# A depthwise convolution's taps dealt anew over VectorE, ScalarE with GpSimd, and TensorE in one trunk kernel

## The chip, the cores and the metric

One core of one Trainium2 chip runs the whole program. The metric is the device time of one launch in microseconds (us); lower is better. The program has no communication with other cores.

## The reference

The model is a trunk of two layers over 256 tokens of width 1024, in float32. Each layer is a half-step SwiGLU feed-forward block, a token mixer and a second feed-forward block, each with an RMSNorm ahead and behind it. The mixer of layer 0 is a convolution module, and the change lies in it alone:

```
u = h @ w_pw1 + b_pw1
u = u[..., :1024] * sigmoid(u[..., 1024:])
c = depthwise_conv(u, w_dw, width 31, centred) + b_dw     # per channel, 31 taps along the tokens
c = silu(layernorm(c, ln_g, ln_b))                        # over the 1024 channels of a token
return c @ w_pw2 + b_pw2
```

The mixer of layer 1 is differential attention. Feed-forward blocks are `(silu(h @ w_gate) * (h @ w_up)) @ w_down`.

## The kernel before

**Products.** Every float32 weight is split into two parts, hi and lo, that TensorE takes at its faster rate, and so is every activation; a product is three matmuls (`mm3`, lines 151 to 154). Weights arrive in jobs of half a megabyte (`issue`, line 107): SyncE starts a DMA into one of 5 `raw` buffers, ScalarE casts it into `wh` (line 113), VectorE subtracts into `wl` (line 114). Twelve split jobs are held (`NW`), and a job is started when the oldest of the twelve is freed, so weights are some three column pairs ahead of their use.

**Stages.** The trunk runs six sub-blocks in order, named a to f in the tile names: feed-forward, convolution (b), feed-forward, feed-forward, attention, feed-forward. The order of instructions on each engine is fixed when the program is built, by a scheduler; `after(...)` and `tc.high_priority()` steer it. Each engine then works strictly through its own list, and waits at the head of it.

**The convolution module** (`conv`, line 414). Channels are on partitions, 8 channel tiles of 128, tokens along the row; a tile is 128 x 256, with 15 zeros at either end so that a tap is a shifted slice.
- *pw1 and gate.* For each tile, TensorE makes a bank with both halves (tiles 0 to 3 through `px` and transposes `py`, tiles 4 to 7 in the two `gu` banks, line 241), ScalarE the sigmoid `sg` (line 439), VectorE `u` (line 450). A tile that TensorE will convolve is split into hi and lo (`us`, `split_to`, lines 272 and 273).
- *Taps of tiles 0 to 3 (`NDV = 4`)* on VectorE, two tiles in turn so that a tap never waits for the one ahead of it: one `tensor_scalar` (line 478) and 30 `scalar_tensor_tensor` (line 474) a tile, `co = u[shifted] * w + co`, all in SBUF: 120 of the latter.
- *Taps of tiles 4 to 7* on TensorE: for four taps at a time (a chunk) ScalarE makes four diagonal matrices of the hi weights (`dg`, line 495), GpSimd those of the lo weights with one `affine_select` (line 496), and TensorE multiplies (`mm3` into `cv`, line 502). There are 8 chunks a tile and three `dg` buffers. Building runs ahead of TensorE by those buffers.
- *LayerNorm sums.* From tiles 4 and 5 a rough mean of every token is taken (`shifts`, line 522), which all tiles are centred on (`centre`, lines 512 and 515); ScalarE squares them (`sq`, line 519). GpSimd adds the centred tiles and squares of five tiles into `sums` (lines 536, 537, 543, 544), VectorE those of the last three (line 552).
- *Statistics.* TensorE spins on 16 products that nobody reads (`w0`, line 232), then multiplies `sums` with ones into `pv` and `pm` (lines 557 and 559); VectorE and GpSimd make the factor, TensorE spreads it (line 172), with 6 and 6 further spins around it, and the bias rows of pw2 go into `accb` (line 287).
- *pw2.* VectorE normalises, ScalarE takes silu, the result is split and TensorE multiplies (`accb`).

PSUM has eight banks here: four `acc`, two `gu`, two `mi`. The centring of a tile stands at a chosen place in VectorE's list (after a tap of tile 3) and the square at a chosen place in ScalarE's (after a chunk of diagonals), which is all that decides what waits behind them:

```
with after(dve), tc.high_priority():
    ... V.tensor_tensor(c, c, shift, ALU.subtract)
sqs[ct] = hp.tile([P, S], F32, tag="sq", name=f"sq{ct}", bufs=2)
with after(act):
    A.activation(sqs[ct], c, AF.Square)
```

Of the kernel before, what the change touches and what calls it, by code (L numbers as in the profile page):

```python
# [18 lines left out]
P = 128  # L19
# [17 lines left out]
NDV = 4  # L37
# [12 lines left out]
def trunk_kernel(  # L50
# [83 lines left out]
    class Weight:  # L134
        """Some k tiles of a weight, in jobs of half a megabyte; w(k) gives hi and lo of tile k."""
# [30 lines left out]
    def spread(ms, rows, name):  # L166
        """rows[i] = ms[:, i]^-1/2, the same in every partition."""
        n = len(rows)
        rs = sp.tile([P, 2], F32, tag="rs2", name=f"rs{name}", bufs=2)
        G.tensor_tensor(rs[:, :n], ms, nhalf[:, :n], ALU.pow)  # L170
        for i in range(n):
            T.transpose(rows[i], rs[:, i:i + 1].to_broadcast([P, P]), ident)
# [55 lines left out]
    def spin(n, name):  # L228
        """n products that nobody reads: an idle tensor engine drops to half its clock."""
# [4 lines left out]
    def proj(w1, w2, f, name):  # L234
        """[w1 tile f | w2 tile f].T @ xT -> one bank [128, 2*S]."""
# [8 lines left out]
    def proj_x(pairs, order, name):  # L244
        """x[tb] @ [w1 | w2] for pairs of weights i, as (tb, i, bank [128 tokens, 2*FC])."""
# [15 lines left out]
    def projs(pairs, name):  # L261
        """(tile number, bank) of each pair of columns."""
# [12 lines left out]
    class Down:  # L275
        """y[tok, D] += s[:, tok].T @ W over k tiles; the tail one token block after the other."""
# [137 lines left out]
    def conv(hp, name):  # L414
# [22 lines left out]
        for ct, ps in lead():  # L437
            sg = sp.tile([P, S], F32, tag="sg", name=f"sg{name}{ct}")
            A.activation(sg, ps[:, 1, :], AF.Sigmoid, bias=par[:, 8 + ct:9 + ct])
            if ct < NDV:  # L440
                t = us[ct] = hp.tile([P, W], F32, tag="u", name=f"u{ct}", bufs=4)
                ends, u = [t], t[:, PAD:PAD + S]
            else:
                ends = ups[ct] = [hp.tile([P, W], F32R, tag="us", name=f"us{ct}{n}", bufs=8) for n in range(2)]
                u = sp.tile([P, S], F32, tag="hf", name=f"u{ct}")
# [5 lines left out]
            if ct >= NDV:  # L451
# [3 lines left out]
        # bias of pw2, as two rows (hi and lo) that its accumulators start with  # L455
# [9 lines left out]
        # taps of the first tiles on DVE, of the others as products with diagonals  # L465
        raw, tap = {}, {}
        for c0 in range(0, NDV, 2):
            for ct in (c0, c0 + 1):
                raw[ct] = hp.tile([P, S], F32, tag="co", name=f"co{ct}", bufs=NDV)
            for t in range(CONVW):  # L470
                for ct in (c0, c0 + 1):
# [4 lines left out]
                    else:  # L476
                        with after(tap[c0 - 1, CONVW - 1] if c0 else None):
                            V.tensor_scalar(c, u[:, 0:S], wdw[:, ct, 0:1], par[:, 16 + ct:17 + ct],
                                            ALU.mult, ALU.add)

        pm = ps_mi.tile([P, 512], F32, tag="mi", name="pm")
        pv = ps_mi.tile([P, 512], F32, tag="mi", name="pv")
        shift = hp.tile([P, S], F32, tag="shift", name="shift", bufs=1)
        sqs = {}

        built = {}

        def diagonals(ct, then=None):
            uh, ul = ups[ct]
            raw[ct] = ps_acc.tile([P, 512], F32, tag="acc", name=f"cv{ct}")[:, :S]  # L490
# [16 lines left out]

        def centre(ct, dve, act):
            with after(dve), tc.high_priority():
                if ct < NDV:  # L510
                    c = raw[ct]
                    V.tensor_tensor(c, c, shift, ALU.subtract)
                else:
                    c = hp.tile([P, W], F32, tag="us", name=f"co{ct}", bufs=8)[:, :S]
                    V.scalar_tensor_tensor(c, raw[ct], par[:, 16 + ct:17 + ct], shift, ALU.add, ALU.subtract)
            co[ct] = c
            sqs[ct] = hp.tile([P, S], F32, tag="sq", name=f"sq{ct}", bufs=2)
            with after(act):
                A.activation(sqs[ct], c, AF.Square)


        def shifts():
            # every token is centred on its mean over two tiles before its variance is taken
            for ct in (4, 5):
                e = sp.tile([P, S], F32, tag="hf", name=f"e{ct}")
                A.activation(e, raw[ct], AF.Identity, bias=par[:, 16 + ct:17 + ct])
                T.matmul(pm[:, S:], ones_d, e, start=ct == 4, stop=ct == 5)
            A.activation(shift, pm[:, S:], AF.Copy, scale=float(KD // 2))

        for ct in range(NDV, KD):  # L530
            diagonals(ct, shifts if ct == 6 else None)
        sums = [hp.tile([P, S], F32, tag=f"sum{n}", name=f"sum{n}", bufs=1) for n in range(2)]
        end = (CONVW - 1) // 4

        def add(ct, E):
            E.tensor_tensor(sums[0], sums[0], co[ct], ALU.add)
            E.tensor_tensor(sums[1], sums[1], sqs[ct], ALU.add)

        for ct, at, tp in ((4, (6, end), 10), (5, (6, end), 10), (0, (7, 1), 10), (1, (7, 1), 10), (6, (7, end), 24)):
            centre(ct, tap[3, tp], built[at][0])  # L540
            with after(built[at][1]):
                if ct == 5:
                    G.tensor_tensor(sums[0], co[4], co[5], ALU.add)
                    G.tensor_tensor(sums[1], sqs[4], sqs[5], ALU.add)
                elif ct != 4:
                    add(ct, G)
        centre(7, tap[3, CONVW - 1], built[7, end][0])
        for ct in (2, 3):
            centre(ct, None, built[7, end][0])
        for n, v in enumerate((co, sqs)):  # L550
            for ct in (7, 2, 3):
                V.tensor_tensor(sums[n], sums[n], v[ct], ALU.add)
# [237 lines left out]
```

## Time and profile before

| | |
|---|---|
| three runs | 1059.96, 1060.96, 1061.01 us; median 1060.96 |
| profiled execution, first to last instruction | span 1059.0 us |
| TensorE busy over the span | 1023.4 us (97%) |
| VectorE, ScalarE, GpSimd busy | 659.6, 553.7, 72.4 us |
| pw1's products end, diagonals begin | 258.97 us |
| first product of pw2 | 326.69 us |

The page gives one figure for the profiled execution, its span; the program's start and end lie around it, so a run of the same kernel is listed about 2 us above it. Spans, starts and lengths below are in us from the first instruction. A row "x30" is 30 instructions run together: its length is from the start of the first to the end of the last. In square brackets stands the idle time ahead of an instruction and what ended it.

### The profile page before, as it was taken

What the parts mean: (1) busy time and instruction counts of PE and PEld (TensorE: products, weight loads), DVE (VectorE), ACT (ScalarE), POOL (GpSimd) and SP (SyncE); (2) the same over time, 40 slices, a digit from 0 to 9 for tenths busy, and PEclk for the clock granted to TensorE, in tenths of its full rate; (3) what the DMA queues carried; (4) which work ended last, traced back from release to release, by engine and by line L of the source; (5) the groups of instructions that cost most, each with busy time, mean ns of one, the idle gap of its engine ahead of it and who ended that gap; (6) DMA issues with size and microseconds to landing.
All of it is one profiled execution on the core that took longest, in us unless ns stands there. A gap on an engine that the chain in (4) does not pass through costs nothing.

```text
span 1059.0 us, 17905 instructions
## 1 busy us (share of the span) xinstructions
PE 1023.4 (97%) x7133; PEld 947.7 (89%) x7133; DVE 659.6 (62%) x1007; ACT 553.7 (52%) x933; POOL 72.4 (7%) x110
## 2 busy tenths in 40 slices
PE   6999999999969999999999999999999999999997
PEld 5899999899967989999989999998899789999995
DVE  6655556679996755455575555566777685555542
ACT  6564445476845644444455445454577665445431
POOL 1000000031560100000010000001000110000000
PEclk9999999999998999999999999999999999999999
DMA  9877465376000666475555665554842255665511
GB/s 296 283 208 221 150 205 179 112 259 197 14 1 0 215 203 218 148 229 177 165 175 185 195 218 151 190 188 133 276 150 91 80 165 180 196 216 155 187 58 40
DMA packets 130492, 177.62 MB, mean 168 GB/s; under 512 B 6173, under 2 KB 112709, under 8 KB 130408
## 3 DMA queue, kind: packets, MB, share of 16 engines
q1 hardware_dynamic: 130408, 176.47, 52.1%
q8 instruction: 56, 0.92, 0.3%
q14 instruction: 28, 0.23, 0.1%
HBM read 175.40 MB, written 1.05 MB: 167 GB/s over the span
## 4 chain that ended last, share of the span: by engine, by line
PE 79%; DVE 10%; issue 3%; ACT 2%; DMA 2%; POOL 2%; SPq 0%; DVEq 0%; POOLq 0%; ACTq 0%
DVE co L474 4%; PE gud L152 3%; PE gua L152 3%; PE gua L154 3%; PE gud L154 3%; PE gud L153 3%; PE gua L153 3%; PE guc L152 3%; PE guf L152 3%; PE guf L154 3%; PE guc L154 3%; PE guc L153 3%; PE guf L153 3%; DVE wl L114 2%; PE accf L152 2%
## 5 line engine op out<-in xcount | busy, mean ns | idle before, releaser
L114 DVE TENSOR_TENSOR wl<-raw,wh 128x1024 fp32r<-128x1024 f32 x320 | 389.7, 1224 | 135.6 <-ACT wh L113 132.8
L113 ACT CAST wh<-raw 128x1024 fp32r<-128x1024 f32 x320 | 333.9, 1051 | 137.0 <-PE accd L154 14.0
L152 PE MATMUL guc<-xTh,wh 128*128 128x256 f32 x288 | 82.1, 285 | 0.0
L152 PE MATMUL guf<-xTh,wh 128*128 128x256 f32 x288 | 82.0, 285 | 0.0
L152 PE MATMUL gud<-xTh,wh 128*128 128x256 f32 x288 | 82.0, 285 | 0.0
L152 PE MATMUL gua<-xTh,wh 128*128 128x256 f32 x288 | 82.0, 285 | 0.0
L154 PE MATMUL guc<-xTh,wl 128*128 128x256 f32 x288 | 81.7, 284 | 0.0
L154 PE MATMUL gua<-xTh,wl 128*128 128x256 f32 x288 | 81.7, 284 | 0.0
L154 PE MATMUL guf<-xTh,wl 128*128 128x256 f32 x288 | 81.7, 284 | 0.0
L154 PE MATMUL gud<-xTh,wl 128*128 128x256 f32 x288 | 81.7, 284 | 0.0
L153 PE MATMUL gua<-xTl,wh 128*128 128x256 f32 x288 | 81.0, 281 | 0.0
L153 PE MATMUL guc<-xTl,wh 128*128 128x256 f32 x288 | 81.0, 281 | 0.0
L153 PE MATMUL guf<-xTl,wh 128*128 128x256 f32 x288 | 80.9, 281 | 0.0
L153 PE MATMUL gud<-xTl,wh 128*128 128x256 f32 x288 | 80.9, 281 | 0.0
L474 DVE SCALAR_TENSOR_TENSOR co<-u,wdw,co 128x256 f32<-128x256 f32 x120 | 61.9, 581 | 0.0
L153 PEld LDWEIGHTS guc<-xTl,wh 128*128 128x128 f32 x288 | 54.7, 190 | 0.5
L153 PEld LDWEIGHTS gua<-xTl,wh 128*128 128x128 f32 x288 | 54.6, 190 | 0.5
L153 PEld LDWEIGHTS guf<-xTl,wh 128*128 128x128 f32 x288 | 54.6, 190 | 0.5
L153 PEld LDWEIGHTS gud<-xTl,wh 128*128 128x128 f32 x288 | 54.6, 190 | 0.5
L152 PEld LDWEIGHTS guc<-xTh,wh 128*128 128x128 f32 x288 | 54.4, 189 | 0.5
L152 PEld LDWEIGHTS gud<-xTh,wh 128*128 128x128 f32 x288 | 54.4, 189 | 0.5
L152 PEld LDWEIGHTS guf<-xTh,wh 128*128 128x128 f32 x288 | 54.4, 189 | 0.5
(357 smaller groups left out, 2672.4 us busy)
## 6 DMA issues: line engine op xcount, KB each, us to landing
raw<-in_ffn_w_gate_dram SPq DMA_DIRECT2D x88, 512.0 KB, 5.1
raw<-in_ffn_w_up_dram SPq DMA_DIRECT2D x88, 512.0 KB, 4.9
raw<-in_ffn_w_down_dram SPq DMA_DIRECT2D x88, 512.0 KB, 4.8
raw<-in_conv_w_pw_dram SPq DMA_DIRECT2D x24, 512.0 KB, 4.5
raw<-in_attn_w_qkv_dram SPq DMA_DIRECT2D x24, 512.0 KB, 4.7
raw<-in_attn_w_o_dram SPq DMA_DIRECT2D x8, 512.0 KB, 4.9
gpre<-in_ffn_norm_pre_dram SPq DMA_DIRECT2D x3, 512.0 KB
x<-in_x_dram SPq DMA_DIRECT2D x2, 512.0 KB
```

The source lines that it names most:

```text
L113: A.copy(hi, raw)
L114: V.tensor_tensor(lo, raw, r32(hi), ALU.subtract)
L152: T.matmul(o, sh, mh, start=first, stop=False)
L153: T.matmul(o, sh, ml, start=False, stop=False)
L154: T.matmul(o, sl, mh, start=False, stop=last)
L474: tap[ct, t] = V.scalar_tensor_tensor(c, u[:, t:t + S], wdw[:, ct, t:t + 1], c, ALU.mult, ALU.add)
```

## The change

Three tiles instead of four stay on TensorE (5, 6, 7). Four stay on VectorE, now tiles 1 to 4, and their running sums lie in two PSUM banks of the `acc` pool instead of SBUF. Tile 0 goes to two other engines: ScalarE makes 31 products `u[shifted] * w` (line 475 of the changed kernel), two to a buffer, and GpSimd adds them two at a time into `part` with 14 additions of 128 x 512 and one of 128 x 256, and folds the two halves with another (lines 477 and 479). There are two product buffers. The centred tiles of the three late tiles are no longer added by VectorE: TensorE multiplies each of them, and its squares, with ones into the same `pm` and `pv`, after the sum of the other five, which GpSimd still adds (line 561). The two rotating pools of tiles, `u` and `us`, become one of 11 (`NU`), centred tiles get buffers of their own from it, and `sq` gets three buffers.

```diff
@@ -34,7 +34,8 @@
 LAM_INIT = 0.8 - 0.6 * math.exp(-0.3)
 NW = 12
 NRAW = 5
-NDV = 4
+NU = 11
+ON_POOL, ON_DVE, ON_PE = 0, (1, 2, 3, 4), (5, 6, 7)
 WARM = (16, 6, 6)
 
 
...
@@ -437,22 +438,22 @@
         for ct, ps in lead():
             sg = sp.tile([P, S], F32, tag="sg", name=f"sg{name}{ct}")
             A.activation(sg, ps[:, 1, :], AF.Sigmoid, bias=par[:, 8 + ct:9 + ct])
-            if ct < NDV:
-                t = us[ct] = hp.tile([P, W], F32, tag="u", name=f"u{ct}", bufs=4)
+            if ct in ON_PE:
+                ends = ups[ct] = [hp.tile([P, W], F32R, tag="u", name=f"us{ct}{n}", bufs=NU) for n in range(2)]
+                u = sp.tile([P, S], F32, tag="hf", name=f"u{ct}")
+            else:
+                t = us[ct] = hp.tile([P, W], F32, tag="u", name=f"u{ct}", bufs=NU)
                 ends, u = [t], t[:, PAD:PAD + S]
-            else:
-                ends = ups[ct] = [hp.tile([P, W], F32R, tag="us", name=f"us{ct}{n}", bufs=8) for n in range(2)]
-                u = sp.tile([P, S], F32, tag="hf", name=f"u{ct}")
             with after(power[0]):
                 for t in ends:
                     G.tensor_copy(t[:, 0:PAD], zero)
                     G.tensor_copy(t[:, PAD + S:], zero)
             V.scalar_tensor_tensor(u, ps[:, 0, :], par[:, ct:ct + 1], sg, ALU.add, ALU.mult)
-            if ct >= NDV:
+            if ct in ON_PE:
                 split_to(*[t[:, PAD:PAD + S] for t in ends], u)
         A.activation(warm, sg[:, 0:1], AF.Silu)
...
@@ -462,32 +463,48 @@
-        # taps of the first tiles on DVE, of the others as products with diagonals
-        raw, tap = {}, {}
-        for c0 in range(0, NDV, 2):
-            for ct in (c0, c0 + 1):
-                raw[ct] = hp.tile([P, S], F32, tag="co", name=f"co{ct}", bufs=NDV)
+        raw, tap, built = {}, {}, {}
+        part = hp.tile([P, 2, S], F32, tag="part", name="part", bufs=1)
+        for t0 in range(0, CONVW, 2):
+            nt = min(2, CONVW - t0)
+            pr = part if t0 == 0 else hp.tile([P, 2, S], F32, tag="prod", name=f"prod{t0}", bufs=2)
+            for i in range(nt):
+                t = t0 + i
+                A.activation(pr[:, i, :], us[ON_POOL][:, t:t + S], AF.Copy, scale=wdw[:, ON_POOL, t:t + 1])
+            if t0:
+                G.tensor_tensor(part[:, :nt, :], part[:, :nt, :], pr[:, :nt, :], ALU.add)
+        raw[ON_POOL] = hp.tile([P, W], F32, tag="u", name="cp", bufs=NU)[:, :S]
+        G.tensor_tensor(raw[ON_POOL], part[:, 0, :], part[:, 1, :], ALU.add)
+        last = None
+        for c0 in range(0, len(ON_DVE), 2):
+            two = ON_DVE[c0:c0 + 2]
+            bank = ps_acc.tile([P, 2, S], F32, tag="acc", name=f"cd{c0}")
+            for n, ct in enumerate(two):
+                raw[ct] = bank[:, n, :]
             for t in range(CONVW):
-                for ct in (c0, c0 + 1):
+                for ct in two:
                     u, c = us[ct], raw[ct]
                     if t:
                         tap[ct, t] = V.scalar_tensor_tensor(c, u[:, t:t + S], wdw[:, ct, t:t + 1], c,
                                                             ALU.mult, ALU.add)
                     else:
-                        with after(tap[c0 - 1, CONVW - 1] if c0 else None):
+                        with after(last):
                             V.tensor_scalar(c, u[:, 0:S], wdw[:, ct, 0:1], par[:, 16 + ct:17 + ct],
                                             ALU.mult, ALU.add)
+            last = tap[two[-1], CONVW - 1]
         pm = ps_mi.tile([P, 512], F32, tag="mi", name="pm")
         pv = ps_mi.tile([P, 512], F32, tag="mi", name="pv")
-        shift = hp.tile([P, S], F32, tag="shift", name="shift", bufs=1)
-        sqs = {}
-        built = {}
-        def diagonals(ct, then=None):
+        shift = sp.tile([P, S], F32, tag="sg", name="shift")
+        def diagonals(ct, pool, tag, then=None):
             uh, ul = ups[ct]
-            raw[ct] = ps_acc.tile([P, 512], F32, tag="acc", name=f"cv{ct}")[:, :S]
+            raw[ct] = pool.tile([P, 512], F32, tag=tag, name=f"cv{ct}")[:, :S]
             for t0 in range(0, CONVW, 4):
                 nt = min(4, CONVW - t0)
                 dg = big(f"dg{ct}_{t0}", F32R).rearrange("p (a t c) -> p a t c", a=2, c=P)
...
@@ -505,58 +522,55 @@
                 if t0 == 0 and then is not None:
                     then()
+        sqs = {}
         def centre(ct, dve, act):
+            co[ct] = hp.tile([P, W], F32, tag="u", name=f"co{ct}", bufs=NU)[:, :S]
             with after(dve), tc.high_priority():
-                if ct < NDV:
-                    c = raw[ct]
-                    V.tensor_tensor(c, c, shift, ALU.subtract)
+                if ct in ON_DVE:
+                    V.tensor_tensor(co[ct], raw[ct], shift, ALU.subtract)
                 else:
-                    c = hp.tile([P, W], F32, tag="us", name=f"co{ct}", bufs=8)[:, :S]
-                    V.scalar_tensor_tensor(c, raw[ct], par[:, 16 + ct:17 + ct], shift, ALU.add, ALU.subtract)
-            co[ct] = c
-            sqs[ct] = hp.tile([P, S], F32, tag="sq", name=f"sq{ct}", bufs=2)
+                    V.scalar_tensor_tensor(co[ct], raw[ct], par[:, 16 + ct:17 + ct], shift, ALU.add, ALU.subtract)
+            sqs[ct] = hp.tile([P, S], F32, tag="sq", name=f"sq{ct}", bufs=3)
             with after(act):
-                A.activation(sqs[ct], c, AF.Square)
+                A.activation(sqs[ct], co[ct], AF.Square)
         def shifts():
-            # every token is centred on its mean over two tiles before its variance is taken
-            for ct in (4, 5):
+            for n, ct in enumerate(ON_PE[:2]):
                 e = sp.tile([P, S], F32, tag="hf", name=f"e{ct}")
                 A.activation(e, raw[ct], AF.Identity, bias=par[:, 16 + ct:17 + ct])
-                T.matmul(pm[:, S:], ones_d, e, start=ct == 4, stop=ct == 5)
+                T.matmul(pm[:, S:], ones_d, e, start=n == 0, stop=n == 1)
             A.activation(shift, pm[:, S:], AF.Copy, scale=float(KD // 2))
-        for ct in range(NDV, KD):
-            diagonals(ct, shifts if ct == 6 else None)
+        p0, p1, p2 = ON_PE
+        diagonals(p0, ps_acc, "acc")
+        diagonals(p1, ps_acc, "acc")
+        diagonals(p2, ps_gu, "gu", shifts)
+        end = (CONVW - 1) // 4
         sums = [hp.tile([P, S], F32, tag=f"sum{n}", name=f"sum{n}", bufs=1) for n in range(2)]
-        end = (CONVW - 1) // 4
-        def add(ct, E):
-            E.tensor_tensor(sums[0], sums[0], co[ct], ALU.add)
-            E.tensor_tensor(sums[1], sums[1], sqs[ct], ALU.add)
-        for ct, at, tp in ((4, (6, end), 10), (5, (6, end), 10), (0, (7, 1), 10), (1, (7, 1), 10), (6, (7, end), 24)):
-            centre(ct, tap[3, tp], built[at][0])
-            with after(built[at][1]):
-                if ct == 5:
-                    G.tensor_tensor(sums[0], co[4], co[5], ALU.add)
-                    G.tensor_tensor(sums[1], sqs[4], sqs[5], ALU.add)
-                elif ct != 4:
-                    add(ct, G)
-        centre(7, tap[3, CONVW - 1], built[7, end][0])
-        for ct in (2, 3):
-            centre(ct, None, built[7, end][0])
-        for n, v in enumerate((co, sqs)):
-            for ct in (7, 2, 3):
-                V.tensor_tensor(sums[n], sums[n], v[ct], ALU.add)
-        # mean of each token in rows (pm) and columns, mean of squares in columns
+        d0, d1, d2, d3 = ON_DVE
+        first = None
+        for ct, at, tp in ((p0, 2, 12), (p1, 2, 12), (ON_POOL, 3, 14), (d0, 4, 16), (d1, 4, 16)):
+            centre(ct, tap[d3, tp], built[p2, at][0])
+            if first is None:
+                first = ct
+            else:
+                with after(built[p2, end][1]):
+                    for n, v in enumerate((co, sqs)):
+                        G.tensor_tensor(sums[n], v[first] if ct == p1 else sums[n], v[ct], ALU.add)
+        centre(p2, tap[d3, 26], built[p2, end][0])
+        for ct in (d2, d3):
+            centre(ct, None, built[p2, end][0])
         spin(WARM[0], "w0")
-        for n in range(2):
-            for tb in range(NTB):
-                T.matmul(pv[:, 2 * n + tb:2 * n + tb + 1], sums[n][:, tb * P:(tb + 1) * P], ones_d[:, 0:1],
-                         start=True, stop=True)
-        T.matmul(pm[:, :S], ones_d, sums[0], start=True, stop=True)
+        parts = [sums] + [(co[ct], sqs[ct]) for ct in (p2, d2, d3)]
+        for i, v in enumerate(parts):
+            T.matmul(pm[:, :S], ones_d, v[0], start=i == 0, stop=i == len(parts) - 1)
+            for n in range(2):
+                for tb in range(NTB):
+                    T.matmul(pv[:, 2 * n + tb:2 * n + tb + 1], v[n][:, tb * P:(tb + 1) * P], ones_d[:, 0:1],
+                             start=i + n + tb == 0, stop=i == len(parts) - 1, skip_group_check=True)
         spin(WARM[1], "w1")
         m2 = sp.tile([P, 4], F32, tag="m2", name="m2", bufs=1)
         V.tensor_copy(m2, pv[:, 0:4])
```

Outside the convolution module no engine's list differs. Inside it three places matter. Numbers behind names are buffer numbers of the build.

The first is ScalarE between the sigmoids `sgb` of tiles 6 and 7, while TensorE still works on pw1. Before:

```order
L439 ACTIVATE sgb_2754<-gub_2705,par 128x256
L272 CAST us_2756<-u_2758 128x256
L113 CAST wh_2817<-raw_2815 128x1024
L113 CAST wh_2823<-raw_2821 128x1024
L113 CAST wh_2829<-raw_2827 128x1024
L113 CAST wh_2835<-raw_2833 128x1024
L439 ACTIVATE sgb_2839<-gub_2766,par 128x256
L453 ACT_TABLE_LOAD
L453 ACTIVATE warm<-sgb_2839 128x1
L272 CAST us_2841<-u_2843 128x256
```

After the change:

```order
L475 ACTIVATE prod_2910<-u_2448,wdw 128x256 x2
L440 ACTIVATE sgb_2748<-gub_2699,par 128x256
L475 ACTIVATE prod_2914<-u_2448,wdw 128x256 x2
L475 ACTIVATE prod_2918<-u_2448,wdw 128x256
L273 CAST us_2750<-u_2752 128x256
L114 CAST wh_2811<-raw_2809 128x1024
L114 CAST wh_2817<-raw_2815 128x1024
L512 ACTIVATE dg_0_3053<-ident,wdh 128x128 x2
L114 CAST wh_2823<-raw_2821 128x1024
L512 ACTIVATE dg_0_3053<-ident,wdh 128x128
L114 CAST wh_2829<-raw_2827 128x1024
L440 ACTIVATE sgb_2833<-gub_2760,par 128x256
```

Products for tile 0 now stand ahead of the split of tile 6, the casts `wh` and the last sigmoid, and three of the four diagonals of tile 5's first chunk (`dg_0`) have moved between the casts. A product buffer is filled again only when GpSimd has added what it held two buffers ago, so the last product buffer (`prod_2918`) waits for the 13th of GpSimd's additions.

The second is ScalarE in the last tile on TensorE (tile 7): its chunks of diagonals, and the squares of the centred tiles (`co` of tile 5 is `co_3484`). Before, the squares of the first two centred tiles stood ahead of tile 7's first chunk:

```order
L495 ACTIVATE dg_24_3394<-ident,wdh 128x128 x4
L495 ACTIVATE dg_28_3412<-ident,wdh 128x128 x3
L519 ACTIVATE sq_3571<-co_3569 128x256
L519 ACTIVATE sq_3575<-co_3573 128x256
L495 ACTIVATE dg_0_3427<-ident,wdh 128x128 x4
L495 ACTIVATE dg_4_3445<-ident,wdh 128x128 x4
L495 ACTIVATE dg_8_3463<-ident,wdh 128x128 x4
L519 ACTIVATE sq_3580<-co_2865 128x256
L495 ACTIVATE dg_12_3481<-ident,wdh 128x128 x4
```

After the change the square of the first stands in the middle of the tile, ahead of its last four chunks:

```order
L512 ACTIVATE dg_8_3378<-ident,wdh 128x128 x4
L512 ACTIVATE dg_12_3396<-ident,wdh 128x128 x3
L544 ACTIVATE shift<-pm 128x256
L512 ACTIVATE dg_12_3396<-ident,wdh 128x128
L536 ACTIVATE sq_3486<-co_3484 128x256
L512 ACTIVATE dg_16_3414<-ident,wdh 128x128 x4
L512 ACTIVATE dg_20_3432<-ident,wdh 128x128 x4
L536 ACTIVATE sq_3490<-co_3488 128x256
L512 ACTIVATE dg_24_3450<-ident,wdh 128x128 x4
L536 ACTIVATE sq_3496<-co_3494 128x256
L512 ACTIVATE dg_28_3468<-ident,wdh 128x128 x3
```

What moved is how much of TensorE's work is behind a centring by VectorE. In VectorE's list the first centring comes after 60 taps of the first pair and 47 of the second, 107 in all, where it came after 84.

The third is TensorE behind the last diagonals: the spins `w`, the products with ones, and the spins after them. Before:

```order
L232 MATMUL w_3611<-xTh 128x512 x16
L557 MATMUL pv<-ones_d,sum_3567 128x1 x2
L557 MATMUL pv<-ones_d,sum_3568 128x1 x2
L559 MATMUL pm<-sum_3567,ones_d 128x256
L232 MATMUL w_3633<-xTh 128x512 x6
L172 MATMUL pv<-ident,rsln 128x128 x2
L232 MATMUL w_3648<-xTh 128x512 x6
```

After the change (the groups for the two last tiles, `co_3516` and `co_3520`, go on as the one for `co_3512`):

```order
L233 MATMUL w_3524<-xTh 128x512 x16
L569 MATMUL pm<-sum_3482,ones_d 128x256
L572 MATMUL pv<-ones_d,sum_3482 128x1 x2
L572 MATMUL pv<-ones_d,sum_3483 128x1 x2
L569 MATMUL pm<-co_3512,ones_d 128x256
L572 MATMUL pv<-ones_d,co_3512 128x1 x2
L572 MATMUL pv<-ones_d,sq_3514 128x1 x2
L569 MATMUL pm<-co_3516,ones_d 128x256
L572 MATMUL pv<-ones_d,co_3516 128x1 x2
L572 MATMUL pv<-ones_d,sq_3518 128x1 x2
```

Two products with 256 columns and eight with one column (each row's matmul is two in the trace) became four times that, and they stand behind the 16 spins as before.

## Rows read from the trace of the kernel before

**Rows 1.** The profile's page: an engine's busy time; costliest groups (busy, mean ns).

```profile
PE 1023.4 (97%) x7133; PEld 947.7 (89%) x7133; DVE 659.6 (62%) x1007; ACT 553.7 (52%) x933; POOL 72.4 (7%) x110
...
L114 DVE TENSOR_TENSOR wl<-raw,wh 128x1024 fp32r<-128x1024 f32 x320 | 389.7, 1224 | 135.6 <-ACT wh L113 132.8
L113 ACT CAST wh<-raw 128x1024 fp32r<-128x1024 f32 x320 | 333.9, 1051 | 137.0 <-PE accd L154 14.0
```

**Rows 2.** Chain that ended last, in order of time, convolution: start, us, what.

```profile
263.43 15.86 DVE co L474 x30
...
280.26 12.16 DVE co L474 x24
...
293.87 15.29 DVE co L474 x24
...
318.02 1.83 PE pv L557 x8
...
320.92 2.56 PE w L232 x6
...
325.57 1.12 PE accb L287 x4
326.69 0.43 PE accb L152
```

**Rows 3.** Timeline of VectorE: start, us, line, operation, tiles, count.

```profile
233.27 0.88 DVE L450 SCALAR_TENSOR_TENSOR u<-py,par,sgb 128x256 f32<-128x256 f32 x2 [0.34 <-ACT sgb L439]
...
261.45 0.48 DVE L450 SCALAR_TENSOR_TENSOR u<-gub,par,sgb 128x256 f32<-128x256 f32 x1
261.84 1.25 DVE L474 SCALAR_TENSOR_TENSOR co<-u,wdw,co 128x256 f32<-128x256 f32 x2
...
309.48 4.83 DVE L474 SCALAR_TENSOR_TENSOR co<-u,wdw,co 128x256 f32<-128x256 f32 x12
```

**Rows 4.** Timeline of GpSimd, in the convolution and in a feed-forward block.

```profile
260.73 2.09 POOL L496 TENSOR_SCALAR_AFFINE_SELECT dg<-wdl 128x512 fp32r<-128x512 f32 x2 [21.05 <-PE cv L154]
...
297.25 1.79 POOL L536 TENSOR_TENSOR sum<-sum,co 128x256 f32<-128x256 f32 x2
...
309.64 5.93 POOL L536 TENSOR_TENSOR sum<-sum,co 128x256 f32<-128x256 f32 x1 [4.32 <-DVE co L515]
315.53 0.72 POOL L537 TENSOR_TENSOR sum<-sum,sq 128x256 f32<-128x256 f32 x1
...
532.96 0.54 POOL L163 TENSOR_TENSOR rsqc<-msqc,nhalf 128x1 f32<-128x1 f32 x1 [173.86 <-DVE msqc L161]
...
545.32 1.38 POOL L163 TENSOR_TENSOR rsqc<-msqc,nhalf 128x1 f32<-128x1 f32 x1 [8.35 <-DVE msqc L161]
```

**Rows 5.** Groups by line and shape on GpSimd: busy, mean ns.

```profile
L496 POOL TENSOR_SCALAR_AFFINE_SELECT dg<-wdl 128x512 fp32r<-128x512 f32 x28 | 22.0, 790 | 46.4 <-PE cv L154 28.5 <-PE py L432 13.6 <-ACT dg L495 4.1
...
L496 POOL TENSOR_SCALAR_AFFINE_SELECT dg<-wdl 128x384 fp32r<-128x384 f32 x4 | 2.6, 642 | 1.7 <-PE cv L154 1.6
```

**Rows 6.** Timeline of ScalarE: sigmoids of tiles 2 and 3, and of tile 7.

```profile
237.85 0.84 ACT L439 ACTIVATE sgb<-py,par 128x256 f32<-128x256 f32 x2
...
260.00 0.47 ACT L439 ACTIVATE sgb<-gub,par 128x256 f32<-128x256 f32 x1
```

**Rows 7.** One line of the attention block on ScalarE: ns min/median/max.

```profile
L676 ACT ACTIVATE tt<-tt,rec x16: 492/506/517, 778.1 to 837.6; 128x256 f32<-128x256 f32 x16
```

**Rows 8.** Timeline of TensorE: products with ones, spins, one-column products in attention.

```profile
282.60 1.02 PE L527 MATMUL pm<-e,ones_d 128*128 128x256 f32 x4
...
307.96 3.81 PE L232 MATMUL w<-xTh 128*128 128x512 f32 x16
...
840.60 0.50 PE L702 MATMUL pn<-ones_e,osq 128*128 128x1 f32 x4
```

**Rows 9.** Stretches: us, busy of PE, PEld, DVE, ACT, POOL, then TensorE's clock, DMA.

```profile
312.00:314.00 2.00, 0.00 (x0) 0.00 (x0) 2.00 (x6) 0.00 (x0) 2.00 (x1) 1.00 0.00 0
...
315.00:324.00 9.00, 5.98 (x19) 5.14 (x20) 5.00 (x18) 1.25 (x3) 1.97 (x3) 0.50 0.00 1
```

## The prediction, made before the changed kernel ran

> **What bounds the kernel now.** I read the page first, then the chain that ended last, then the engines' timelines in the convolution. TensorE is busy 97% of the span [rows 1], so only a place where it waits can be worth something. The chain leaves TensorE in one stretch: from 263.4 to 314 it runs through VectorE's taps, then through the sums, the products with ones and the spins, and comes back to full products at 326.69 [rows 2]. Tiles 4 to 7 on TensorE are done by 307.96, where the 16 spins begin [rows 8]. So the stage ends with VectorE's taps. Everything behind 326.69 should only shift, as its lists are unchanged.
>
> Why the taps are slow is in the timelines. Twelve taps alone take 4.83: with 0.47 for the last, 0.396 apart [rows 3]. But 78 taps of the chain take 43.3 [rows 2], where 0.396 each would make 30.9: **12.4 us are lost while GpSimd works beside them.** GpSimd loses too: an addition that needs 0.72 alone took 5.93 beside taps running without a gap [rows 4].
>
> **What the change removes.** The taps stay 120 in number and gain no cost that a row shows: `u` reads PSUM and is 0.40 apart from the next (0.88 for two, 0.48 for the last) [rows 3]. A write to PSUM by VectorE stands nowhere in the trace. Bounds: 0.396, as nothing of the size was faster, and 0.48, if the next waits out the whole length. I take 0.396, nearest to the `u` row. That GpSimd no longer slows them rests on one place: while two selects ran from 260.73 on [rows 4], `u` with one operand in PSUM took its usual 0.48 and the next two taps, all SBUF, took 1.25 instead of 0.87 [rows 3]. [...]
>
> Gone as well are VectorE's six late sums. They fill most of the 3.7 between the taps' end at 314.3 [rows 3] and the products with ones at 318.02 [rows 2]; I count 2.5.
>
> **What it adds ahead of the taps' end.** 31 products on ScalarE at 0.51, some 0.41 apart (the length of the same operation, with 16 of it in a row) [rows 7], replace 31 diagonals. They are fed to GpSimd through two buffers, and *ScalarE's list has casts, splits and sigmoids behind them*, so GpSimd's pace becomes that of ScalarE, and through the sigmoid that of VectorE.
> - The first addition starts at 239.2: sigmoids of tiles 2 and 3 until 238.6 [rows 6], then a product.
> - An addition of 128 x 512 has no row. Bounds: 0.72, that of half the size, and 1.44, twice it [rows 4]. Selects need 642 ns for 384 and 790 for 512 columns [rows 5], so about 0.2 is fixed; 0.52 x 2 + 0.2 is 1.24. I take 1.3, as each waits for the one ahead.
> - VectorE's weight splits, 1.22 long [rows 1], read two SBUF operands and delay GpSimd: a power of 0.54 took 1.38 beside one [rows 4]. Four of them fall among the additions: 4 x 0.84 = 3.4.
> - The 13th addition so ends at 239.2 + 16.9 + 3.4 = 259.5. Only then does ScalarE pass the last product (0.4), a split (0.3), four casts of 1.05 [rows 1] and three diagonals (0.9, an estimate from the product's 0.41 for twice the columns): the sigmoid of tile 7 starts at 265.3, where it was 260.0 [rows 6]. Tile 7's `u` came 1.45 behind it [rows 3, 6]; two weight splits whose casts come late now stand ahead and meet GpSimd, 0.7 each: 268.2 instead of 261.45 [rows 3].
>
> In VectorE's list 21 taps stand ahead of that `u`, where 28 did. The first centring is behind tap 107: from 268.2, `u`, a split and the pair's two first taps (four of about 0.4, 1.5) and 86 taps x 0.396 (34.1) make **303.8**. Without the late start it would be near 296.
>
> TensorE is not on this path until then: `gu` waits about 2 for tile 5's `u`, diagonals begin near 263 for 259, and two tiles and half the third are done by about 297. GpSimd's selects behind its additions cost TensorE a few us there, all ahead of 303.8.
>
> **What it adds behind.** ScalarE's square of tile 5 stands ahead of tile 7's last four chunks. From 303.8: centring 0.5 (as long as `u`) [rows 3], the square and a first diagonal some 0.4 each: TensorE resumes at 305.1 with 45 matmuls. A matmul of 256 columns is half a spin's 0.234 (3.81 for 16) [rows 8], 0.12: 5.4. TensorE idled some 8 us. In the trace it idled from 311.8 [rows 8] to 318 [rows 2]; the clock was 1.00 from 312 to 314 and 0.50 from 315 to 324 [rows 9], 3.1 us past the first dense spins at 320.92 [rows 2]. So the 45 lose between 0 and 5.4; I take half of about 3.5, 1.8. Tile 7 ends at 312.3.
>
> The 16 spins, which ran in slack, now stand on the path: 3.7, to 316.0. GpSimd's eight sums (after the last select, 0.72 each) end near 315 and hide under them; if they took 1 us each they would show. Then four groups: two matmuls of 0.21 and eight of 0.12 [rows 8], 1.4 each, 5.6: **321.6**. Before, eight at half clock ended at 318.02 + 1.84 = 319.86 [rows 2]. So the statistics start 1.7 later.
>
> But TensorE comes to them at full clock. Before, 6.8 passed from 319.86 to 326.69, most at half clock [rows 2, 9]. At full clock: VectorE's three small steps and GpSimd's power 1.4 (an estimate: a power alone is 0.54 [rows 4], the steps and hand-overs as much again and more), spreading 0.2, six spins 1.4 [rows 8], bias 1.1 [rows 2]: 4.2 rounded up, the first six spins lying beside. Bounds 4.2 and 6.8. I take 4.2: pw2 starts at 325.8 for 326.69.
>
> **Sum:** 0.9 us earlier on a profiled span of 1059.0; the listed runs lie 1 to 2 above that span, their median at 1060.96, so **1060.1**. Gross: 12.4 and 2.5 saved, some 7 lost to the late start, 3.7 of spins, 4 of groups and 1.8 of clock put on the path, 2.6 of clock won back behind. A difference under 0.2%, 2.1 us, can't be told from none here. The forecast's own range is 1058.8 to 1063.0.
>
> **Rivals.**
> *Faster.* The additions cost 1.1 and meet splits less than I count: tile 7's `u` comes 3 earlier, TensorE idles less. For it: every POOL step may hide its start beside a split. Against: 1.38 against 0.54 [rows 4]. It gives 301 for 303.8: 1057.3, and 1056 with no clock loss. It decides when the first centring falls before about 302.5.
>
> *Slower by PSUM.* A tap that writes PSUM costs more. At 0.44 the 86 taps add 3.8, 1063.9; at the full 0.48 7.2, 1067.3. From 0.43 on it is slower than before. Against it is only the read row [rows 3]. [...]
>
> *Slower by the queue.* Additions at 1.44, each collision paid on VectorE too: the first centring falls at 307.5, 1063.8.
>
> *The sums in PSUM don't part the engines.* Then taps beside selects still take 0.53, as the 30 from 263.43 did [rows 2]: 11 us over 86 taps, less while the selects wait for TensorE, 8: 1068. The one `u` beside selects speaks against it.
>
> **How the numbers follow.** Forecast 0.37, faster 0.28, slower by PSUM 0.17, by the queue 0.12, engines not parted 0.06. That is faster 0.28, same 0.37, slower 0.35. The range runs from 1056.5, near the faster rival's end, to 1067.5, the PSUM rival's; a tenth lies out at either side.
>
> **What would show it.** Right: taps 0.40 apart throughout; GpSimd's 14 additions near 1.3, ending about 264; tile 7's sigmoid near 266; VectorE idle for several us between 242 and 268; a gap on TensorE of 5 to 9 us in tile 7, a half clock behind it, and the 16 spins directly ahead of the groups. Wrong: taps at 0.43 or more; GpSimd done by 260; TensorE never waiting for the square; or the half clock lasting through the statistics, which alone adds up to 2.6 and as much on the groups.

## The result, and the profile after

The changed kernel took **1072.39 us** (median of 4 runs, 1070.95 to 1073.07), the kernel before 1060.46 beside it (1059.93 to 1061.01): ratio 1.0111, 95% interval 1.0097 to 1.0125. That is 1.1% slower, clear of the spread of the runs. Forecast were 1060.1 and a range up to 1067.5.

| | before | after |
|---|---|---|
| span of the profiled run, us | 1059.0 | 1068.9 |
| tile 7's `u` on VectorE | 261.45 | 268.39 |
| taps behind that `u` | 92 | 99 |
| VectorE's last centring ended | 315.38 | 324.84 |
| first product of pw2 on TensorE | 326.69 | 336.97 |
| pw2's first product to the end | 732.3 | 731.9 |

The loss lies in the convolution, ahead of pw2, as pw2 begins 10.3 us later and the span is 9.9 longer. Timeline of VectorE after, whose like of before is in [rows 3] and, for the long runs of taps, in the chain of [rows 2]:

```profile
247.94 0.48 DVE L492 SCALAR_TENSOR_TENSOR cd<-u,wdw,cd 128x256 f32<-128x256 f32 x1
248.34 2.01 DVE L115 TENSOR_TENSOR wl<-raw,wh 128x1024 fp32r<-128x1024 f32 x1
...
268.39 0.47 DVE L451 SCALAR_TENSOR_TENSOR u<-gub,par,sgb 128x256 f32<-128x256 f32 x1
268.78 1.00 DVE L492 SCALAR_TENSOR_TENSOR cd<-u,wdw,cd 128x256 f32<-128x256 f32 x2
...
270.03 19.38 DVE L492 SCALAR_TENSOR_TENSOR cd<-u,wdw,cd 128x256 f32<-128x256 f32 x37
...
290.48 24.64 DVE L492 SCALAR_TENSOR_TENSOR cd<-u,wdw,cd 128x256 f32<-128x256 f32 x47
315.02 0.87 DVE L533 SCALAR_TENSOR_TENSOR co<-cv,par,shift 128x256 f32<-128x256 f32 x2
...
316.87 6.78 DVE L492 SCALAR_TENSOR_TENSOR cd<-u,wdw,cd 128x256 f32<-128x256 f32 x13
...
324.10 0.74 DVE L531 TENSOR_TENSOR co<-cd,shift 128x256 f32<-128x256 f32 x2
```

The last centring before (timeline of VectorE):

```profile
314.91 0.47 DVE L515 SCALAR_TENSOR_TENSOR co<-cv,par,shift 128x256 f32<-128x256 f32 x1
```

How to read a pitch (the time from one start to the next) out of it: 47 taps in 24.64 with 0.48 for the last are (24.64 - 0.48) / 46 = **0.525 apart**, where 0.396 was counted on. The first 37 ran beside GpSimd's selects, most of the others alone; both stand at 0.525, so it isn't GpSimd. One tap takes hardly longer than before (0.48 to 0.49 for 0.47), and behind the single tap at 247.94 a split of weights started 0.40 later: the price falls in the main between two taps. Timelines of GpSimd and ScalarE after [rows 4, 6]:

```profile
238.81 8.13 POOL L477 TENSOR_TENSOR part<-part,prod 128x512 f32<-128x512 f32 x6 [0.43 <-ACT prod L475]
...
262.64 1.60 POOL L479 TENSOR_TENSOR cp<-part 128x256 f32<-128x256 f32 x1
...
279.59 0.63 POOL L513 TENSOR_SCALAR_AFFINE_SELECT dg<-wdl 128x512 fp32r<-128x512 f32 x1 [0.92 <-PE cv L155]
```

```profile
265.72 0.46 ACT L440 ACTIVATE sgb<-gub,par 128x256 f32<-128x256 f32 x1
...
315.54 0.42 ACT L536 ACTIVATE sq<-co 128x256 f32<-128x256 f32 x1 [19.25 <-DVE co L533]
```

The engines did part: a select beside taps takes 0.63, where it was 0.79 on average before [rows 5], and six additions took 8.13, 1.35 each. ScalarE's square waited 19.25 for the first centring, and TensorE behind it (timeline of TensorE after; [rows 8] are the spins before):

```profile
255.24 0.52 PE L153 MATMUL gub<-xTh,wh 128*128 128x256 f32 x1 [2.22 <-DVE u L451]
...
316.30 0.58 PE L153 MATMUL cv<-us,dg 128*128 128x256 f32 x1 [16.70 <-ACT dg L512]
...
323.50 3.81 PE L233 MATMUL w<-xTh 128*128 128x512 f32 x16
327.15 0.60 PE L569 MATMUL pm<-sum,ones_d 128*128 128x256 f32 x2
...
332.37 1.62 PE L233 MATMUL w<-xTh 128*128 128x512 f32 x6
...
336.97 0.50 PE L153 MATMUL accb<-wh,z 128*128 128x512 f32 x1
```

So why does VectorE's last centring end 9.5 us later? Tile 7's `u` is 6.9 later. The 99 taps behind it take 1.00 + 19.38 + 24.64 + 6.78 = 51.8, where the 92 took 49.4 before [rows 2, 3]: those were 0.54 apart on average, most of them beside GpSimd, and these are 0.52 apart, for something else. So the one price took the place of the other, and seven taps more make 2.4. From the last centring to pw2 it is 12.1 for 11.3, another 0.8.

### The profile page after: what moved, and what is told of

It reads as the page before. It is cut to its first block, busy times and chain, and to the rows that moved or that the text cites. A ratio compares the mean times of both kernels' runs of the same rounds, so it can differ in the third digit from the quotient of the medians.

```text
span 1068.9 us, 17785 instructions
## 1 busy us (share of the span) xinstructions
PE 1019.5 (95%) x7070; PEld 943.8 (88%) x7070; DVE 658.5 (62%) x1000; ACT 555.8 (52%) x932; POOL 80.8 (8%) x116
## 3 DMA queue, kind: packets, MB, share of 16 engines
HBM read 175.40 MB, written 1.05 MB: 165 GB/s over the span
## 4 chain that ended last, share of the span: by engine, by line
PE 77%; DVE 10%; issue 4%; ACT 4%; DMA 3%; POOL 2%; SPq 0%; POOLq 0%; DVEq 0%; ACTq 0%
DVE cd L492 4%; PE gua L153 3%; PE gua L155 3%; PE gua L154 3%; PE guc L153 3%; PE guf L153 3%; PE gud L153 3%; PE guc L155 3%; PE gud L155 3%; PE guf L155 3%; PE guf L154 3%; PE gud L154 3%; PE guc L154 3%; DVE wl L115 3%; DMA raw<-in_ffn_w_gate_dram 2%
## 5 line engine op out<-in xcount | busy, mean ns | idle before, releaser
L492 DVE SCALAR_TENSOR_TENSOR cd<-u,wdw,cd 128x256 f32<-128x256 f32 x120 | 58.7, 489 | 3.8
L153 PEld LDWEIGHTS gua<-xTh,wh 128*128 128x128 f32 x288 | 54.4, 189 | 0.5
```

The source lines that it names most:

```text
L153: T.matmul(o, sh, mh, start=first, stop=False)
L492: tap[ct, t] = V.scalar_tensor_tensor(c, u[:, t:t + S], wdw[:, ct, t:t + 1], c, ALU.mult, ALU.add)
```

## Experiments

Two theories of the 0.13 us per tap had to be parted (PSUM as such, or one bank), and with them the queue of ScalarE and what stands behind the taps. A third was not thought of when the runs were planned: that the program itself makes a tap wait for the one ahead. It is settled below, from the waits in the built programs and from the traces.

**e1, the operand in PSUM and the sums in SBUF.**

```diff
+            elif ct in ON_DVE:
+                t = us[ct] = ps_acc.tile([P, 512], F32, tag="acc", name=f"u{ct}")
...
-            bank = ps_acc.tile([P, 2, S], F32, tag="acc", name=f"cd{c0}")
+            for ct in two:
+                raw[ct] = hp.tile([P, S], F32, tag="cd", name=f"cd{ct}", bufs=4)
...
+        cv = ps_gu.tile([P, 2, S], F32, tag="gu", name="cv56")
```

> The operand in PSUM and the sums in SBUF, the other way round than the change has it; tiles 5 and 6 of TensorE share a bank, 20 spins for 16, and the scheduler puts the first centring after 88 taps (first ones counted) for 111. Theory A (the price is for sums that are read and written back in PSUM, not for reading PSUM): taps 0.396 apart, also beside the selects, so the taps and centrings behind tile 7's u (268.4) end near 311 to 313 for 324.8, TensorE hardly waits for a square, the last of the four groups ends near 315 for 332.4: 1053 to 1058 us against 1072.4. Rival B (any tap that touches PSUM pays): taps 0.52 apart, about 13 us more behind tile 7's u, 1066 to 1070. Rival C (one SBUF operand is enough to contend with GpSimd): taps 0.53 beside the selects and 0.40 else, selects longer than 0.64.

Measured: 1055.18 (1054.6 to 1058.0), ratio to before 0.9953 (0.9941 to 0.9966). Timeline of VectorE in e1:

```profile
269.57 13.40 DVE L496 SCALAR_TENSOR_TENSOR cd<-u,wdw,cd 128x256 f32<-128x256 f32 x34
...
283.80 9.47 DVE L496 SCALAR_TENSOR_TENSOR cd<-u,wdw,cd 128x256 f32<-128x256 f32 x24
```

(13.40 - 0.47) / 33 is 0.392, beside the selects. Rivals B and C fall: reading PSUM cost a tap nothing here (0.396 apart before, in SBUF), and taps with one operand in SBUF didn't contend with GpSimd's selects, which took 0.63 to 0.64 beside them.

**e2, the same with later centrings.** `(p0, 2, 12) ... (d1, 4, 16)` became `(p0, 2, 22) ... (d1, 4, 22)`.

> As e1_u_psum, with the centrings held back to where the change has them (after 108 taps), and the squares behind tile 7's last diagonals in ScalarE's order. VectorE doesn't wait for shift, so its last centring comes 1 to 2 us earlier than in e1, GpSimd's sums start later but still end before it. Theory A: last group near 314, 1052 to 1057. If the time between VectorE's end and the products is set by GpSimd's sums: 1 to 3 us slower than e1.

1056.17 (1054.41 to 1057.11), ratio 0.9960 (0.9947 to 0.9973): not to be told from e1. VectorE's last centring did end 0.9 earlier (310.93 against 311.83); pw2 began at 320.67 in both.

**e3, a measurement.** Tile 0's products are left out, and the sums are placed in two ways:

```diff
+                    side[ct] = hp.tile([P, S], F32, tag="cs", name=f"cs{ct}", bufs=2)
+            else:
+                    raw[ct] = side[ct] = ps_acc.tile([P, 512], F32, tag="acc", name=f"ce{ct}")[:, :S]
...
+                        new, old = (side[ct], c) if t % 2 else (c, side[ct])
```

> A measurement, not a candidate: tile 0's products and additions are left out (its output is the operand itself), the sums of tiles 1 and 2 go to and fro between PSUM and SBUF from tap to tap, those of tiles 3 and 4 stay in PSUM, each in a bank of its own. Theory A1 (a tap that reads a bank waits out the write of the tap ahead to the same bank): tiles 3 and 4 at 0.396, tiles 1 and 2 0.52 at the one step in four that reads PSUM right behind a write of it, mean 0.43. A2 (a read of PSUM waits out any write of PSUM ahead): tiles 3 and 4 at 0.52, tiles 1 and 2 as in A1. A3 (every write to PSUM costs 0.13): tiles 3 and 4 at 0.52, tiles 1 and 2 at a mean of 0.46, every second step long. By the queue theory tile 7's u, at 268.4 with the change, stands at 261 to 263 here, as nothing on ScalarE waits for GpSimd; if something else held it, it stays within 1 of 268.

Timeline of VectorE in e3 (`cs` is SBUF, `cd` the bank that two sums share, `ce` a bank for each sum):

```profile
238.25 0.87 DVE L488 SCALAR_TENSOR_TENSOR cs<-u,wdw,cd 128x256 f32<-128x256 f32 x2
239.16 1.02 DVE L488 SCALAR_TENSOR_TENSOR cd<-u,wdw,cs 128x256 f32<-128x256 f32 x2
240.21 0.87 DVE L488 SCALAR_TENSOR_TENSOR cs<-u,wdw,cd 128x256 f32<-128x256 f32 x2
...
259.81 0.48 DVE L451 SCALAR_TENSOR_TENSOR u<-gub,par,sgb 128x256 f32<-128x256 f32 x1
...
281.19 9.49 DVE L488 SCALAR_TENSOR_TENSOR ce<-u,wdw,ce 128x256 f32<-128x256 f32 x24
```

Taps on sums in banks of their own: (9.49 - 0.48) / 23 = 0.392 apart, though each reads and writes PSUM. On the shared bank, by the starts: read behind read 0.39 (0.87 - 0.48); write behind read 0.52 (0.91 - 0.39); write behind write 0.53 (1.02 - 0.49); read behind write 0.52 (1.05 - 0.53). Three of the four steps pay, not one, so A1 was too narrow about the step: a step paid here (0.52 to 0.53 for 0.39) when two taps in a row touched the same bank and one of them wrote it, even in its other half. A2 and A3 fall. But the steps differ in one thing more. **In the built program the three that pay carry a wait for the tap directly ahead**, on VectorE's own semaphore, as the two sums are halves of one PSUM tile; the free step carries none, and the taps on `ce` wait for the tap two places ahead, the last on their own sum. A tap with such a wait started 0.03 to 0.04 after the end of the one ahead (238.25 + 0.87 = 239.12, and the next started at 239.16). So the wait and the bank can't be parted here. And tile 7's `u` stood at 259.81, 8.6 earlier than with the change and a little below the 261 to 263 expected: nothing held ScalarE up.

**e4, the change with its squares behind tile 7's diagonals, and 78 spins.**

```diff
-            centre(ct, tap[d3, tp], built[p2, at][0])
+            centre(ct, tap[d3, tp], built[p2, end][0])
```

> The change with its squares of tiles 5, 6, 0, 1 and 2 behind tile 7's last diagonals in ScalarE's order, and 78 spins for 16. Taps stay 0.52 apart and the last centring stays near 324.8. TensorE no longer waits 16.7 us inside tile 7, which ends near 304.5, and the groups start near 323.5. Theory (the wait for the square and what is queued behind it, half clock, 16 spins, groups, cost what stands behind VectorE's end): the last group ends near 327.2 for 332.4, 1067 us against 1072.4. Rival (VectorE's last centring and the squares behind it set the groups anyway): within 1 us of 1072.

1070.39 (1069.42 to 1074.0), ratio 1.0104 (1.0085 to 1.0123): 2.0 under the change in the medians instead of 5, and not to be told from it by these runs. TensorE didn't wait inside tile 7, and the groups started at 321.85, but the last came at half clock (timeline, then stretches with the granted clock third from the end):

```profile
321.85 0.60 PE L569 MATMUL pm<-sum,ones_d 128*128 128x256 f32 x2
...
326.04 0.94 PE L569 MATMUL pm<-co,ones_d 128*128 128x256 f32 x2
...
328.34 2.91 PE L233 MATMUL w<-xTh 128*128 128x512 f32 x6
```

```profile
326.00:328.00 2.00, 2.00 (x11) 1.88 (x10) 0.29 (x1) 0.00 (x0) 0.00 (x0) 0.58 0.00 0
328.00:330.00 2.00, 2.00 (x7) 1.71 (x7) 1.29 (x8) 0.00 (x0) 0.71 (x1) 0.50 0.00 0
```

The last group ended at 328.3 for 332.4, 4.0 earlier, where 5.2 were expected. From there to pw2 it took 6.5 for 4.6 at half clock, so pw2 began at 334.84, 2.1 before the change's. The profile so bears the theory in its direction, and the clock took back 1.9 of it; the run times don't exclude the rival.

**e5 and e6, a pair: one bank for two sums, or a bank each.** Both have TensorE's tiles 5 and 6 in one bank (the `cv` line of e1), which frees two; e6 adds

```diff
-            bank = ps_acc.tile([P, 2, S], F32, tag="acc", name=f"cd{c0}")
-            for n, ct in enumerate(two):
-                raw[ct] = bank[:, n, :]
+            for ct in two:
+                raw[ct] = ps_acc.tile([P, 512], F32, tag="acc", name=f"cd{ct}")[:, :S]
```

> The change, but with TensorE's tiles 5 and 6 in the two halves of one bank, as e6 has it: nothing else is edited, and the two sums of a pair of VectorE's still share a bank. The scheduler now puts the first centring after 88 taps. It is the other half of a pair with e6. Theory A1 (same bank): taps 0.52 apart, some 98 steps behind tile 7's u (268.4), so VectorE's last centring ends near 322, the last group near 326: 1064 to 1068 us. If the order and not the taps made the change slow: within 2 us of e6.

> As e5, and each of VectorE's four sums in a bank of its own, so that taps in turn write different banks. Theory A1: taps 0.396 apart, also beside the selects (one operand in PSUM still), VectorE's last centring ends near 311, the last group near 315: 1054 to 1058 us, 9 to 12 less than e5. Rival (every tap on sums in PSUM pays when GpSimd works as well): taps stay over 0.45, and it is within 4 us of e5.

e5: 1068.40 (1068.08 to 1069.1), ratio 1.0075 (1.0057 to 1.0094). e6: 1057.41 (1055.15 to 1060.21), ratio 0.9978 (0.9964 to 0.9991). The 11.0 us between them come from where the sums lie, as the first centring stands at the same place in both (behind 84 of these taps). VectorE in e5, then in e6:

```profile
269.96 19.38 DVE L492 SCALAR_TENSOR_TENSOR cd<-u,wdw,cd 128x256 f32<-128x256 f32 x37
...
290.42 12.57 DVE L492 SCALAR_TENSOR_TENSOR cd<-u,wdw,cd 128x256 f32<-128x256 f32 x24
...
323.62 0.76 DVE L531 TENSOR_TENSOR co<-cd,shift 128x256 f32<-128x256 f32 x2
```

```profile
269.01 0.47 DVE L451 SCALAR_TENSOR_TENSOR u<-gub,par,sgb 128x256 f32<-128x256 f32 x1
...
284.34 9.49 DVE L491 SCALAR_TENSOR_TENSOR cd<-u,wdw,cd 128x256 f32<-128x256 f32 x24
295.90 0.88 DVE L532 SCALAR_TENSOR_TENSOR co<-cv,par,shift 128x256 f32<-128x256 f32 x2 [2.08 <-ACT shift L543]
...
312.57 0.74 DVE L530 TENSOR_TENSOR co<-cd,shift 128x256 f32<-128x256 f32 x2
```

The same 24 taps take 12.57 and 9.49. In e6 VectorE even waits 2.08 for `shift`. In the built programs 105 of e5's 120 taps (108 in the change) wait for the one directly ahead, and each of the change's 108 started 0.035 after its end; in e6 one of 120 does, on its own sum, and of the others a tap started 0.07 to 0.09 before the one ahead had ended. Each tile of e6 is a bank too, so whether one bank costs anything without the wait was tested by no run. Between e5 and the change, where in both two sums share a tile, lie 4.0 us: they differ in the bank of TensorE's tiles 5 and 6, and by it in the order (84 taps ahead of the first centring for 107).

**e7, e6 with half of tile 0's products moved back.** Eight pairs stay ahead; of the others one stands behind every second chunk of diagonals of tiles 5 and 6:

```diff
                 built[ct, t0 // 4] = (ai, gi)
+                if t0 // 4 % 2 and later:
+                    pair(later.pop(0), ai)
```

> As e6, and of tile 0's 16 pairs of products only 8 stand ahead in ScalarE's order, the others one behind every second chunk of diagonals of tiles 5 and 6. Queue theory (GpSimd's additions hold ScalarE up, and through its sigmoids VectorE): the sigmoid of tile 7 goes from about 265.5 to 258 to 260, u of tile 7 from 268.4 to about 260.5, and as VectorE has the same work behind it, its last centring from 311 to 303 to 305; then TensorE's tile 7, near 305 too, sets the groups: 1047 to 1052 us. Rival (additions between the selects hold TensorE's diagonals up by as much): tile 7 of TensorE ends at 308 or later, 1053 to 1056.

**1050.00** (1047.78 to 1052.76), ratio 0.9903 (0.9879 to 0.9927), 7.4 under e6. ScalarE, then VectorE:

```profile
260.75 0.46 ACT L441 ACTIVATE sgb<-gub,par 128x256 f32<-128x256 f32 x1
```

```profile
263.86 0.47 DVE L452 SCALAR_TENSOR_TENSOR u<-gub,par,sgb 128x256 f32<-128x256 f32 x1
...
305.31 0.75 DVE L540 TENSOR_TENSOR co<-cd,shift 128x256 f32<-128x256 f32 x2
```

The queue was real: sigmoid and `u` of tile 7 are 5 earlier, VectorE's end 7.3 (5.2 of `u`, 2.1 of the wait for `shift`). TensorE's tile 7, expected near 305, ended at 297.1 and didn't set the groups: the third group waited for VectorE's centring (timeline of TensorE):

```profile
305.78 1.22 PE L579 MATMUL pm<-co,ones_d 128*128 128x256 f32 x2 [1.56 <-DVE co L540]
```

`u` came 3 later than I expected, as splits of weights stand ahead of it in VectorE's list.

**e8, e6 with the late sums on VectorE again**, and one group of products.

```diff
+                V.tensor_tensor(sums[n], sums[n], v[ct], ALU.add)
...
-        parts = [sums] + [(co[ct], sqs[ct]) for ct in (p2, d2, d3)]
+        parts = [sums]
```

> As e6, with one part of the change undone: the late tiles' six sums are VectorE's again, and one group of products for four. Against e6: three groups less, 4 us, of which two stand in time that TensorE waits anyway; six additions of 0.34 to 0.6 and a hand-over more behind VectorE's end, 2.5. Expected within 1.5 us of e6, either way. If the products with ones were worth the 2.5 that the sums cost before: 2 to 3 us slower.

1055.28 (1053.44 to 1056.07), ratio 0.9949 (0.9931 to 0.9966). The interval just meets e6's, and 1.5 of the difference in the profiled runs is there before the taps end, so it says nothing sure.

**e9 and e10, e7 with e8's edit, with 16 and with 44 spins.**

> e7 with e8's edit: the late tiles' six sums on VectorE, one group of products for four. e8 was 2 us under e6 in the medians, in runs that spread over 5, and both ran their groups at half clock (1.3 us for 0.6). If that is the groups' price, it is 1 to 3 us under e7 here too: 1047 to 1049. If it was the spread of the runs: within 1 us of e7's 1050.

> As e9 with 44 spins for 16, so that TensorE has no idle time between tile 7 (297) and VectorE's last sum (near 309), instead of some 7 us of it. Theory: it comes to the sums' products at full clock, which are then 1.3 us for 2.7, and the spreading and the bias products behind them are full too: 1 to 3 us under e9. Rival: behind the products the path runs through VectorE's and GpSimd's small steps, which the clock doesn't touch: within 1 us of e9.

e9: 1049.66 (1046.7 to 1052.02), ratio 0.9899 (0.9878 to 0.9919), not to be told from e7. e10: 1047.61 (1046.4 to 1050.74), ratio 0.9877 (0.9852 to 0.9901), inconclusive against e9. At the place itself it did what was expected (TensorE in e9, then in e10):

```profile
308.02 1.22 PE L582 MATMUL pm<-sum,ones_d 128*128 128x256 f32 x2 [0.79 <-DVE sum L578]
...
316.22 0.40 PE L154 MATMUL accb<-wh,z 128*128 128x512 f32 x1
```

```profile
297.98 10.15 PE L234 MATMUL w<-xTh 128*128 128x512 f32 x44
...
309.18 0.70 PE L582 MATMUL pm<-sum,ones_d 128*128 128x256 f32 x2
...
314.16 0.50 PE L154 MATMUL accb<-wh,z 128*128 128x512 f32 x1
```

From the sums' products to pw2 it is 8.2 and 5.0 us. But pw2's start to the end was 730.8 in e9's profiled run and 734.8 in e10's: in that stretch, whose lists are the same, the two profiled runs differ by 4.0, more than is won, and e10's was the slowest of its four. Why they do stays open.

## Why the prediction was wrong

**One term failed: the tap that writes PSUM.** It said "I take 0.396, nearest to the `u` row", with 0.48 as the upper bound, "if the next waits out the whole length". The taps were 0.525 apart: 86 of them before the first centring are 86 x 0.129 = 11.1 us more, and the first centring came at 315.02 for 303.8, 11.2 later. Two faults are in that step. The `u` row shows a read of PSUM behind an instruction that it needn't wait for, which was free in e1 and e3 too (0.392 and 0.39 apart); it says nothing of taps on two sums in one PSUM tile, 108 of which wait in the program for the one ahead. That wait was put at nothing, without a reason. And the length of an instruction was taken for the worst case of its pitch; behind such a wait the next started 0.035 after its end, so 0.48 is no bound. With 0.525 in the sum the forecast would have been 1071.2.

Rows of the kernel before already had that gap, in SBUF. In the statistics the two steps `m<-m` each wait for the one ahead, and at lengths of 0.16 the starts are 0.19 to 0.20 apart (timeline of VectorE before):

```profile
319.89 0.16 DVE L562 COPY m<-pv 128x4 f32<-128x4 f32 x1 [1.68 <-PE pv L557]
320.09 0.16 DVE L563 TENSOR_TENSOR m<-m 128x2 f32<-128x2 f32 x1
320.28 0.16 DVE L564 SCALAR_TENSOR_TENSOR m<-m 128x2 f32<-128x2 f32 x1
```

So the gap of 0.03 to 0.04 came with the wait, in SBUF as in PSUM. In the change it stands where e6's taps overlap by 0.085 (medians over all taps), which makes 0.12 of the 0.13 us; for the rest a tap took 0.490 instead of 0.476.

The rival, slower by PSUM, had the right sign and place, too small a price and another cause. The measured price is 129 to 133 ns a tap where two sums share a tile (0.525 against 0.396 and 0.392), and none with a bank each. Taps that read PSUM without that wait were 0.392 apart, in e1 as in e6.

**The rest of the sum held.** Each against the trace after:
- GpSimd parted from VectorE: yes (0.63 for a select, 0.525 with and without it). That rival falls.
- Additions 1.3 each: 1.35, and 2 where a weight split ran beside; the last ended at 262.57 and the fold behind it at 264.24, forecast about 264.
- Sigmoid of tile 7 at 265.3, its `u` at 268.2: 265.72 and 268.39. TensorE's wait for `u` of about 2: 2.22.
- From the first centring to TensorE's next product 1.3: 1.28. The rest of tile 7 with its clock loss 7.2: 316.30 to 323.50, 7.2.
- Spins 3.7 on the path: 3.65. Groups 5.6: 5.2. From there to pw2 4.2: 4.6. The half clock had gone by then, as forecast: 0.50 from 304 to 320, 1.00 from 322 on.

One size follows from the late taps: TensorE's gap in tile 7, foretold as 5 to 9, was 16.70.

So the place and the order were right, and the sign was lost by one wait and its price. That the price comes of two sums in one PSUM tile, and not of PSUM as such or the order, is shown by e5 against e6; that it comes by the wait, by the waits in the programs and the gaps behind them; that one bank costs anything without it isn't shown. The forecast's own verdict for a tap at 0.396, no difference, is not quite shown: e6 has it at 1057.4, but there the scheduler also puts the first centring 23 taps earlier. That order was worth 4.0 between the change and e5; added to e6's time, an estimate for the change in its own order with a bank each is 1061.4.

## What to carry to other kernels

Before sums are kept in PSUM by VectorE, give two sums that are worked on in turn a tile (here a bank) each: 24 taps took 9.49 us so, and 12.57 with both in one tile, where each waits for the one ahead. Look in the built program for whom an instruction waits, not only in the kernel's text. Where a change puts an engine's work into a queue, price what stands behind it in that queue; half of tile 0's products moved back was worth 7.4 us. And an operation that no row shows has no upper bound in its own length: leave room for the next one to start after its end (0.035 behind it here).

## What the runs showed of the hardware

- VectorE started a tap before the one ahead had ended (0.396 apart before, 0.392 in e1, e3 and e6, at 0.47 to 0.48 each), and 0.03 to 0.04 after its end where the program made it wait for that one: the change's taps on two sums in one PSUM tile (0.525 apart at 0.49) as much as the small steps in SBUF before (0.19 to 0.20 apart at 0.16). What a shared bank does without the wait was not tried.
- An operand or a sum in PSUM cost a tap nothing by itself: 0.392 apart in e1 (the operand) and in e6 (the sum), 0.396 with both in SBUF before.
- VectorE's taps with one operand in SBUF and GpSimd's selects didn't hold each other up: in e1 0.392 apart and 0.63 to 0.64 long, beside each other.
- TensorE's clock fell with no idle time to speak of: in e4, after 78 spins at 1.00, it was 0.58 between 326 and 328 and 0.50 behind, while groups of products with ones ran from 321.85 on (TensorE busy 1.86 of 2.00 from 322 to 324, all of the time to 330); in the change the same four groups, from 327.15 to 332.4, ran at 1.00. In e10, with one group, it stayed at 1.00 from 296 to 320. What decides was not tried.
